# A causal mask added in PSUM by VectorE instead of by TensorE, and an output stage cut in the middle

## The chip, the core and the metric

The kernel runs on one core of a Trainium2 chip. The metric is the device time of one execution in microseconds. The core has five engines, each with a queue of its own that is worked off in order: TensorE (PE in the profile; its weight loads are PEld), VectorE (DVE), ScalarE (ACT), GpSimd (POOL) and SyncE (SP), which issues the transfers (DMA). TensorE's products go to PSUM, which has eight banks of 512 float32 columns on 128 partitions; the other working memory is SBUF.

## What is computed

Two layers on 512 tokens of width 1024. Each layer normalises, modulates, projects the tokens once, runs three causal token mixers (A: sparse attention over top-k keys, B: sliding window, C: stick-breaking), gates and merges them, and adds the projected result to the stream. A last norm follows. The change is in mixer C and in the end of the last layer. From the reference, cut down:

```python
def stick_breaking_attention(q, k, v):       # A[t,s] = beta_ts * prod_{s<j<t}(1-beta_tj), s < t
    ...
    strict = (key_pos[None, :] < qpos[:, None])[None, None]
    z = jnp.einsum('bthd,bshd->bhts', qb, k) * (dh ** -0.5)
    log_beta = jax.nn.log_sigmoid(z)
    log_1m = jnp.where(strict, jax.nn.log_sigmoid(-z), 0.0)
    after = lax.cumsum(log_1m, axis=3, reverse=True) - log_1m
    a = jnp.where(strict, jnp.exp(log_beta + after), 0.0)
    return jnp.einsum('bhts,bshd->bthd', a, v)
...
for l in range(DEPTH):
    h = hybrid_layer(h, ...)                 # ends in x + gate * (merged @ w_out)
return rms_norm(h, final_g)
```

Mixer C has 8 heads of width 64.

## The kernel before

All activations lie transposed, features on partitions and tokens in the free dimension. A float32 product is made of three products of rounded operands (high by high, high by low, low by high), so each 128 x 512 output tile of a projection from 1024 features takes 24 products (`ttile`), collected in a `ps_z` bank (3 of them). Weights come by DMA to `wstage` and are split into `whi` and `wlo` by VectorE, ScalarE or GpSimd.

**Order of the work.** The program is first written down by generators that are woven together (`Weave`, `SPACE` holds the spacing constants), and not issued. `Recorder` keeps every operation with the engines that could do it. Its `price` (line 337) gives each a cost per engine, `forward` (410) runs a list schedule over the five engines and the limited buffers, `latest` (544) works back when each operation has to run, which sets the priorities of the next round, and `order` (572) keeps the best of five rounds. `emit` issues that order; so nearly every instruction has line 596 in the profile, and the packed products line 594. The queue of each engine is therefore fixed when the kernel is built; at run time an instruction waits for its operands, and everything behind it on its engine waits too.

**Mixer C** (`c_qk`, 1166) works on pairs of heads, four pairs a layer. For one pair the scores of all four query blocks of 128 fill five `ps_s` banks (of which there are five): a bank per head for block 3 (512 keys), a bank per head for blocks 2 and 0 (384 and 128), and one for block 1 of both (`apos`). TensorE makes eight score products, one correction for the low parts, and seven packed ones (`low_parts`, 64 rows each); for pairs 1 to 3 the value products of the pair before ride in the same run (`value_run`). Before the change each score product was followed by a product of a bf16 identity with a bf16 mask, which adds -2^100 where a key is not before its query, on the last 128 columns. Then, for each bank: absolute value (ScalarE or VectorE), two ScalarE functions, VectorE's min-and-subtract, VectorE's scan from the right, an exponential on ScalarE. `softmax_tr` (1303) transposes the result on TensorE (20 pieces of 128 x 128 into five `ps_s` banks), and a copy brings each bank to SBUF. The next pair needs those five banks again. In the same stage run the projections of the coming pairs, the weight splits, and the top-k search of mixer A (`MAX`, `MATCH_REPLACE` on `score`), which only mixer A needs.

**Mixer A** has the same score code without a mask product (its mask is added by VectorE when a bank is read).

**The end** (`out_phase`, 1463). Output tiles 0 to 5 are computed at full width; tiles 6 and 7 in two parts along the tokens, 320 and 192 in the last layer. `update` adds the product to the old stream (`xm`), squares, collects the squares in `m2` (tile name `m`), and scales by the final gain. `after` forms the norm: a product with minus ones sums over partitions (`rstd`), ScalarE takes logarithm and exponential, once into PSUM for VectorE and once into `zs` for GpSimd; then eight multiplies per part (tiles 2 and 4 on GpSimd, the others on VectorE) and the stores, eight for the first part and four for the second.

**Constants.** `load_consts` (1612) brings rope tables, masks and the bf16 identity and mask at about 47 us.

## Time and profile before

| | us |
|---|---|
| median of 3 runs (lowest, highest) | 1167.84 (1166.76, 1167.96) |
| profiled execution | 1167.66 |
| its span, first to last instruction | 1165.8 |
| TensorE busy | 1154.7 |
| VectorE busy | 969.6 |
| ScalarE busy | 546.6 |
| GpSimd busy | 148.1 |
| granted TensorE clock, mean | 0.999 |

A busy TensorE is not one at its peak: products are pipelined, so the duration of one is longer than the distance to the next, and that distance is what a product costs in a stream. In a timeline row the columns are start, length of the group, engine, line, operation, out<-in, shapes and count; a bracket tells how long the engine sat idle before, and what ended that. Tile names have no buffer numbers: all score banks are `ps_s`.

### The profile page before, as it was taken

Reading aid. Unit: us, or ns where it says so; the run is one execution under the profiler, and the core shown is the slowest. Engines: PE = TensorE matmul, PEld = TensorE weight load, DVE = VectorE, ACT = ScalarE, POOL = GpSimd, SP = SyncE. Lnnn points to the kernel's source line nnn. Section 1 sums busy time; section 2 is a strip of 40 time slices with the busy share of each in tenths; the row PEclk is TensorE's granted clock in tenths of the full one; section 3 lists DMA queues with packets and bytes.
Section 4 is the critical chain, followed back from the end, with each engine's and each line's share of the span. In section 5 each row is a group of like instructions: output and inputs, shape, how many; then the busy total and the mean of one; then the engine's idle time right before and its main releaser. Section 6 shows DMA issues by size and latency. Waiting matters only on the chain.

```text
span 1165.8 us, 17663 instructions
## 1 busy us (share of the span) xinstructions
PE 1154.7 (99%) x5955; PEld 964.1 (83%) x5955; DVE 969.6 (83%) x2221; ACT 546.6 (47%) x1151; POOL 148.1 (13%) x198
## 2 busy tenths in 40 slices
PE   8999999999999999999999999999999999999997
PEld 6899777888888887788889987778888888877886
DVE  7967999999898987778687599999998988566765
ACT  5623766652555642432134157664545665242222
POOL 0100343421000100000000015443100010000000
PEclk9999999999999999999999999999999999999999
DMA  9744322443334445356544432234333333333342
GB/s 350 231 117 122 100 73 82 115 118 111 109 111 124 128 139 142 96 131 180 167 120 110 125 100 82 82 91 125 110 100 107 95 90 100 100 83 91 100 128 98
DMA packets 80539, 139.40 MB, mean 120 GB/s; under 512 B 10048, under 2 KB 20544, under 8 KB 80448
## 3 DMA queue, kind: packets, MB, share of 16 engines
q1 hardware_dynamic: 79296, 136.17, 40.2%
q10 hardware_dynamic: 1152, 2.10, 0.5%
q8 instruction: 47, 0.77, 0.3%
q14 instruction: 44, 0.36, 0.1%
HBM read 125.39 MB, written 4.19 MB: 111 GB/s over the span
## 4 chain that ended last, share of the span: by engine, by line
PE 98%; DVE 1%; DMA 1%; SPq 0%; ACT 0%; issue 0%; DVEq 0%
PE ps_z L596 74%; PE ps_s L596 19%; PE ps_s L594 4%; PE ps_z L594 2%; DMA Y<-in_w_ss 1%; DVE t L596 0%; SPq L596 0%; DVE Y L596 0%; DVE xm L596 0%; DVE e L596 0%; DVE wlo L596 0%; ACT zs L596 0%; DVE whi L596 0%; DVE m L596 0%; ACT ps_s L596 0%
## 5 line engine op out<-in xcount | busy, mean ns | idle before, releaser
L596 PE MATMUL ps_z<-uh,whi 128*128 128x512 f32 (+1 forms) x905 | 355.0, 394 | 0.0
L596 PE MATMUL ps_z<-uh,wlo 128*128 128x512 f32 (+1 forms) x905 | 351.9, 390 | 0.0
L596 PE MATMUL ps_z<-ul,whi 128*128 128x512 f32 (+1 forms) x905 | 351.2, 389 | 0.0
L596 DVE TENSOR_TENSOR wlo<-wstage,whi 128x512 fp32r<-128x512 f32 (+2 forms) x299 | 195.4, 656 | 14.3 <-ACT whi L596 4.9
L596 PEld LDWEIGHTS ps_z<-uh,wlo 128*128 128x128 f32 x905 | 169.9, 188 | 34.9 <-issue 0.7
L596 PEld LDWEIGHTS ps_z<-uh,whi 128*128 128x128 f32 x905 | 169.8, 188 | 34.8 <-issue 1.7
L596 PEld LDWEIGHTS ps_z<-ul,whi 128*128 128x128 f32 x905 | 169.9, 188 | 33.2 <-issue 0.3
L596 DVE CAST whi<-wstage 128x512 fp32r<-128x512 f32 (+2 forms) x215 | 88.0, 410 | 124.3 <-PE ps_z L596 103.8
L596 POOL TENSOR_TENSOR wlo<-wstage,whi 128x512 fp32r<-128x512 f32 (+2 forms) x73 | 93.4, 1282 | 391.9 <-DVE whi L596 87.5
L596 ACT CAST whi<-wstage 128x512 fp32r<-128x512 f32 (+1 forms) x124 | 74.1, 602 | 143.4 <-PE ps_z L596 128.9
L596 PE MATMUL ps_z<-Y,whi 128*128 128x512 f32 x384 | 119.1, 391 | 0.0
L596 ACT ACTIVATE e<-ps_z 128x512 f32<-128x512 f32 x68 | 40.5, 595 | 121.3 <-PE ps_z L596 121.0
L596 PEld LDWEIGHTS ps_z<-Y,whi 128*128 128x128 f32 x384 | 71.6, 188 | 14.6
L596 ACT ACTIVATE t<-t 128x512 f32<-128x512 f32 x120 | 69.4, 626 | 17.7 <-DVE t L596 16.8
L596 ACT ACTIVATE e<-e 128x512 f32<-128x512 f32 x96 | 59.8, 631 | 36.5 <-DVE e L596 36.0
L596 PE MATMUL ps_z<-Y,wlo 128*128 128x512 f32 x192 | 74.8, 389 | 0.0
L596 ACT ACTIVATE t<-t,nm 128x256 f32<-128x256 f32 (+3 forms) x128 | 65.0, 510 | 9.8 <-DVE nm L596 9.7
L596 PEld LDWEIGHTS ps_s<-small,t 128*128 128x128 f32 x432 | 50.4, 140 | 7.4
L596 PE MATMUL ps_s<-small,t 128*128 128x128 f32 x432 | 56.3, 273 | 0.0
L596 DVE MAX8 m<-score 128x8 f32<-128x256 f32 (+2 forms) x96 | 53.1, 555 | 1.2
L596 DVE MATCH_REPLACE8 score<-m,score 128x256 f32<-128x256 f32 (+2 forms) x96 | 52.0, 542 | 0.0
L596 PE MATMUL ps_s<-KH,Q 128*128 128x256 f32 (+3 forms) x280 | 50.6, 308 | 0.0
(219 smaller groups left out, 1938.3 us busy)
## 6 DMA issues: line engine op xcount, KB each, us to landing
wstage<-in_w_t SPq DMA_DIRECT2D x212, 256.0 KB, 2.7
wstage<-in_w_v SPq DMA_DIRECT2D x48, 182.0 KB, 2.4
m<-zs SPq DMA_DIRECT2D x128, 64.0 KB, 2.0
wstage<-in_w_gt SPq DMA_DIRECT2D x32, 256.0 KB, 2.7
wstage<-in_w_ss SPq DMA_DIRECT2D x32, 256.0 KB, 2.7
wstage<-in_w_o SPq DMA_DIRECT2D x32, 256.0 KB, 2.7
Y<-in_w_ss SPq DMA_DIRECT2D x15, 512.0 KB, 5.7
wstage<-in_w_first SPq DMA_DIRECT2D x16, 256.0 KB, 3.9
```

Of the source, the lines that this page charges most:

```text
L594: self.real[engine].matmul(*[real(a) for a in q[:3]], start=q[3], stop=True, skip_group_check=True)
L596: made = getattr(self.real[engine], y.op)(*[real(a) for a in y.args], **{k: real(v) for k, v in y.kw.items()})
```

## The change

1. Mixer C: the eight mask products of each block go. Instead VectorE adds the float32 mask to the bank in PSUM, in front of the absolute value: 128 columns for the two banks of block 3, 256 for the two banks of blocks 2 and 0 (their masked columns are neighbours), and two times 128 for the bank of block 1. The bf16 identity and mask, their casts and one staging tile go; the float32 mask is loaded to a tile of its own.
2. The end of the last layer: the parts are 256 and 256. The eight multiplies of a part are a function of their own (`last`). Those of the first part are recorded behind the updates of the second part, those of the second part at the very end. The first part uses GpSimd for tiles 1, 3 and 5 and buffers `Y`; both parts store two tiles with one transfer, four transfers each.
3. The planner: a product of under about 235 columns is priced at 0.112 us at least; a store to the output no longer holds up later transfers in the model; and the latest start of an operation counts its full latency.

```diff
-                c = 4 * n / 2.4e3 + 0.01 if rhs.dtype == F32 else 0.06 if rhs.dtype == BF16 else (n + 33.5) / 2.4e3
+                c = 4 * n / 2.4e3 + 0.01 if rhs.dtype == F32 else 0.06 if rhs.dtype == BF16 else max(0.112, (n + 33.5) / 2.4e3)
...
-                x.end = dma_free = max(at + (2.1 if at < 20.0 else 3.0), dma_free) + y.lag * (1.2 if dma_free < 5.5 else 1.0)
+                if not x.writes:
+                    x.end = at + 2.1
+                else:
+                    x.end = dma_free = max(at + (2.1 if at < 20.0 else 3.0), dma_free) + y.lag * (1.2 if dma_free < 5.5 else 1.0)
...
-        late = {x.i: end - x.hold for x in out}
+        late = {x.i: end - max(x.hold, x.end - x.start) for x in out}
...
                 for e in range(2):
                     mm(o[e], q[:, e, ts], kh[:, e, :W], first[e])
-                for e in range(2):
-                    mm(o[e][:, W - 128:], ident_b, cmask_b, False)
                 if i == 1:
                     mm(o[1], q[:, 1, ts], kl[:, S:], False)
             low_parts(q, kl, apos, zb, "c", p, LOW_ALL)
             for bk in (0, 3, 1, 4, 2):
                 z = zb[bk]
+                if bk % 3:
+                    m = z[:, 256:].rearrange("p (a b) -> p a b", a=2) if bk != 2 else z.rearrange("p (a b) -> p a b", a=2)[:, :, 128:]
+                    DVE.tensor_tensor(out=m, in0=m, in1=cmask.unsqueeze(1).to_broadcast([P, 2, P]), op=OP.add)
+                else:
+                    DVE.tensor_tensor(out=z[:, 384:], in0=z[:, 384:], in1=cmask, op=OP.add)
                 t = pt[bk] = t512("t", 10)
...
+        def last(cs_):
             w = cs_.stop - cs_.start
             for d in range(KT):
-                if d % 2 == 0 or w > S // 2:
-                    o, n = t512("t", 10), 0
-                v, a = o[:, n:n + w], st["xn"][d][:, cs_]
-                n += w
-                if d in (2, 4):
+                if d % 2 == 0:
+                    o = rec.tile("Y", [P, 2 * S], F32) if cs_.start == 0 else t512("t", 10)
+                v, a = o[:, w * (d % 2):w * (d % 2) + w], st["xn"][d][:, cs_]
+                if d in ((1, 3, 5) if cs_.start == 0 else (2, 4)):
                     POOL.tensor_tensor(out=v, in0=a, in1=st["rstd_sb"][:, cs_], op=OP.mult)
                 else:
                     DVE.tensor_tensor(out=v, in0=a, in1=st["rstd"][:, cs_], op=OP.mult)
-                if w > S // 2:
-                    SP.dma_start(out[:, d, cs_], v)
-                elif d % 2:
-                    SP.dma_start(out[:, d - 1:d + 1, cs_], o[:, :n].rearrange("p (a b) -> p a b", a=2))
+                if d % 2:
+                    SP.dma_start(out[:, d - 1:d + 1, cs_], o[:, :2 * w].rearrange("p (a b) -> p a b", a=2))
...
-            for cs_ in HALVES if l + 1 < L else (slice(0, 320), slice(320, S)):
+            parts = HALVES if l + 1 < L else (slice(0, 256), slice(256, S))
+            for cs_ in parts:
                 for i in range(2):
                     mms(6 + i, ws[2 * i:2 * i + 2], z[i], cs_)
                     update(6 + i, z[i], xr[i], cs_)
+                if cs_.start and l + 1 == L:
+                    last(parts[0])
                 after(cs_)
+            if l + 1 == L:
+                last(parts[1])
```

How the planner's order moves, at three places.

TensorE's queue at the first score block of mixer C in layer 0, before and then changed (`KH` keys, `Q` queries, `klow` low parts, `ps_z` a projection that runs around the block):

```order
L596 MATMUL ps_z_1370<-uh3_370,wlo_1300 128x512
L596 MATMUL ps_s_1397<-KH_1375,Q_1323 128x512
L596 MATMUL ps_s_1399<-KH_1375,Q_1323 128x512
L596 LDWEIGHTS ident_b_86
L596 MATMUL ps_s_1397<-cmask_b_87,ident_b_86 128x128
```

```order
L599 MATMUL ps_z_1366<-uh3_368,wlo_1296 128x512
L599 MATMUL ps_s_1393<-KH_1371,Q_1319 128x512
L599 MATMUL ps_s_1395<-KH_1371,Q_1319 128x512
L599 MATMUL ps_s_1398<-KH_1371,Q_1319 128x384
L599 MATMUL ps_s_1400<-KH_1371,Q_1319 128x384
L599 MATMUL ps_s_1398<-KH_1371,Q_1319 128x128
L599 MATMUL ps_s_1400<-KH_1371,Q_1319 128x128
L599 MATMUL ps_s_1409<-KH_1371,Q_1319 128x256 x2
```

The mask products, two behind each pair of score products, are gone; nothing else in the block moved but the correction with `klow`, which now follows the packed ones.

VectorE's queue behind the second score block of the same layer, before and then changed (`e` the gated value products of the pair before, `Y` its split, rows with 128x511 the scans):

```order
L596 TENSOR_TENSOR e_1686<-ps_z_1664,G_649 128x512
L596 TENSOR_SCALAR t_1692<-ps_s_1633 128x512
L596 TENSOR_SCALAR t_1700<-ps_s_1635 128x512
L596 TENSOR_TENSOR Y_1695<-e_1686,Y_1695 128x512
L596 TENSOR_SCALAR t_1712<-ps_s_1646 128x512
L596 SCALAR_TENSOR_TENSOR t_1683<-ps_s_1622,t_1683 128x512
L596 SCALAR_TENSOR_TENSOR t_1690<-ps_s_1624,t_1690 128x512
L596 MEMSET t_1683 128x1
L596 SCALAR_TENSOR_TENSOR t_1683<-ps_s_1622,t_1683 128x511
```

```order
L599 TENSOR_TENSOR e_1663<-ps_z_1637,G_645 128x512
L599 TENSOR_TENSOR ps_s_1608<-ps_s_1608,cmask_86 128x128
L599 CAST Y_1670<-e_1663 128x512
L599 TENSOR_TENSOR ps_s_1612<-ps_s_1612,cmask_86 128x128
L599 TENSOR_TENSOR Y_1670<-e_1663,Y_1670 128x512
L599 TENSOR_TENSOR ps_s_1614<-ps_s_1614,cmask_86 128x256
L599 TENSOR_TENSOR ps_s_1619<-ps_s_1619,cmask_86 128x256
L599 TENSOR_SCALAR t_1694<-ps_s_1614 128x512
L599 TENSOR_SCALAR t_1700<-ps_s_1619 128x512
L599 SCALAR_TENSOR_TENSOR t_1672<-ps_s_1608,t_1672 128x512
L599 SCALAR_TENSOR_TENSOR t_1681<-ps_s_1612,t_1681 128x512
L599 SCALAR_TENSOR_TENSOR t_1672<-ps_s_1608,t_1672 128x511
```

Four additions stand ahead of the first scan; the fifth (128x2x128) comes behind the fourth scan, with two search steps, a replacement and two low parts of keys between it and the last scan. From `e` to the last scan there are 17 rows before and 25 now. On TensorE the last four transposes of this block now stand behind 21 more products in three runs, where it was five in two, and 3 products ahead of the next block, where it was 19.

VectorE's queue at the end of the kernel, before and then changed (`xm_12108` and `xm_12079` are tile 7, `xm_12077` and `xm_12049` tile 6):

```order
L596 TENSOR_TENSOR m2_11831<-m2_11831,e_12148 128x192
L596 TENSOR_TENSOR t_12159<-xm0_11824,ps_s_12132 128x320
L596 TENSOR_TENSOR t_12168<-xm1_11868,ps_s_12132 128x320
L596 TENSOR_TENSOR t_12175<-xm3_11958,ps_s_12132 128x320
L596 TENSOR_TENSOR t_12182<-xm5_12043,ps_s_12132 128x320
L596 TENSOR_TENSOR t_12185<-xm6_12077,ps_s_12132 128x320
L596 TENSOR_TENSOR t_12188<-xm7_12108,ps_s_12132 128x320
L596 SCALAR_TENSOR_TENSOR xm7_12108<-ps_z_12074,mods1_77,G_12054 128x192
L596 TENSOR_TENSOR e_12195<-xm7_12108 128x192
```

```order
L599 TENSOR_TENSOR Y_12114<-xm0_11796,ps_s_12098 128x256
L599 SCALAR_TENSOR_TENSOR xm6_12049<-ps_z_12011,mods1_77,G_11982 128x256
L599 TENSOR_TENSOR Y_12124<-xm2_11885,ps_s_12098 128x256
L599 TENSOR_TENSOR Y_12130<-xm4_11973,ps_s_12098 128x256
L599 TENSOR_TENSOR Y_12138<-xm6_12049,ps_s_12098 128x256
L599 TENSOR_TENSOR Y_12138<-xm7_12079,ps_s_12098 128x256
L599 TENSOR_TENSOR m2_11803<-m2_11803,e_12127 128x256
L599 SCALAR_TENSOR_TENSOR xm7_12079<-ps_z_12046,mods1_77,G_12027 128x256
L599 TENSOR_SCALAR xm7_12079<-xm7_12079,small_69 128x256
```

The first part's multiplies on VectorE are five instead of six, and four of them now stand behind the second part's update of tile 6; the square of the last tile is no longer on VectorE. On TensorE the product that sums the first norm stands behind 63 of the 96 products of tiles 6 and 7, where it stood behind 69.

More of the change, by code (lines that the diff above doesn't have):

```diff
@@ L1608, in start @@
         ada_load(2)
-    sin_t = cos_t = tri0 = band = ident_b = cmask_b = None
+    sin_t = cos_t = tri0 = band = cmask = None
     def load_consts():
-        nonlocal sin_t, cos_t, tri0, band, ident_b, cmask_b
+        nonlocal sin_t, cos_t, tri0, band, cmask
         late = f(st["uh"][4][:, 0:1])
@@ L1622, in load_consts @@
         tri0, band = cb[:, 0:512], cb[:, 512:768]
-        cc = t512("t", 10)[:, :128]
-        POOL.tensor_copy(out=cc[:, 0:1], in_=late)
-        SP.dma_start(cc, consts[:, 768:896])
-        ident_b = fixed("ident_b", [P, P], BF16)
-        POOL.tensor_copy(out=ident_b, in_=ident)
-        cmask_b = fixed("cmask_b", [P, P], BF16)
-        POOL.tensor_copy(out=cmask_b, in_=cc[:, :P])
+        cmask = fixed("cmask", [P, P], F32)
+        POOL.tensor_copy(out=cmask[:, 0:1], in_=late)
+        SP.dma_start(cmask, consts[:, 768:896])
     def one(fn):
```

## The prediction, made before the changed kernel ran

> **What bounds the kernel now.** I read the busy shares on the first page of the profile, then the chain that ended last.
>
> ```profile
> PE 1154.7 (99%) x5955; PEld 964.1 (83%) x5955; DVE 969.6 (83%) x2221; ACT 546.6 (47%) x1151; POOL 148.1 (13%) x198
> PE 98%; DVE 1%; DMA 1%; SPq 0%; ACT 0%; issue 0%; DVEq 0%
> ```
>
> TensorE is busy for 1154.7 of 1165.8 us, and 98% of the chain runs through it. Idle time is left at the start and in the last 9 us. So a microsecond taken from TensorE's stream is a microsecond gained, as long as nothing else begins to make it wait. VectorE gets the new work, so I asked for busy time in stretches of 20 us: the second stick-breaking block, the sliding-window mixer after it, and the end.
>
> ```profile
> 140.00:160.00 20.00, 20.00 (x115) 15.60 (x114) 19.76 (x39) 14.80 (x27) 9.09 (x16) 1.00 0.34 94
> 300.00:320.00 20.00, 20.00 (x97) 16.76 (x96) 16.25 (x45) 12.49 (x34) 1.29 (x1) 1.00 0.40 119
> ```
>
> The columns are TensorE, its weight loads, VectorE, ScalarE, GpSimd, then the granted clock (1.00). In the stick-breaking stage VectorE has 0.24 us free in 20. It is full, though TensorE does not wait for it: much of what it does there is due later. That is the danger of this change: work goes from the engine that bounds the kernel to the one that has no room at that very place.
>
> **The mask products on TensorE.** The sparse mixer's score block is the same code shape without the mask: eight score products, one low part of 256 columns, seven packed low parts. The chain of waits in order of time has both, first a stick-breaking block (17 instructions ahead of the packed ones), then a sparse one (9); columns are start and length in us.
>
> ```profile
> 140.88 2.06 PE ps_s L596 x17
> 143.72 2.30 PE ps_z L594 x16
> 342.10 1.38 PE ps_s L596 x9
> 344.26 16.54 PE ps_z L596 x72
> ```
>
> From block start to the first instruction after the packed low parts: 2.84 us with the mask (140.88 to 143.72), 2.16 without (342.10 to 344.26). Eight mask products cost 0.68 us, and there are eight blocks (4 head pairs, 2 layers): **-5.4 us**. Bounds: at most 5.6 if a block varies by 0.02; nothing at all if TensorE comes to wait for VectorE at these places (a rival below). The nearest group row prices it otherwise:
>
> ```profile
> L596 PE MATMUL ps_s<-cmask_b,ident_b 128*128 128x128 bf16 x64 | 9.1, 224 | 0.0
> ```
>
> 224 ns is the latency of one pipelined product; 64 of them would be 14 us, which the block comparison rules out. The Trainium skill (TensorE: Matmul & The Clock Gate, Back-to-back issue gap) gives 56 ns from start to start for an isolated 128-column bf16 product and about 81 ns in a stream with weight loads; an estimate from that page for 64 products is 3.6 to 5.2 us. By the page the sum below would come out 0.2 to 1.8 us smaller; the block comparison exceeds both, as it also holds what the change of type costs its neighbours.
>
> **More interruptions by transposes.** In the changed order 63 runs of transposes stand between other products, where 58 stood. What one costs shows behind the second block's scans:
>
> ```profile
> 156.98 1.58 PE L596 MATMUL ps_s<-small,t 128*128 128x128 f32 x13
> 158.31 0.48 PE L596 MATMUL ps_z<-uh,whi 128*128 128x512 f32 x1
> 159.09 0.49 PE L596 MATMUL ps_s<-small,t 128*128 128x128 f32 x3
> 159.34 0.47 PE L596 MATMUL ps_z<-uh,whi 128*128 128x512 f32 x1
> 159.66 0.40 PE L596 MATMUL ps_z<-ul,whi 128*128 128x512 f32 x1
> 159.89 0.60 PE L596 MATMUL ps_s<-small,t 128*128 128x128 f32 x4
> 164.66 0.61 PE L596 MATMUL ps_s<-KH,Q 128*128 128x512 f32 x2
> ```
>
> The product behind a run lasts 0.32 us from start to start (159.34 to 159.66) where its neighbours take 0.23 (159.66 to 159.89). Five more runs by 0.09: **+0.45 us**.
>
> **The additions on VectorE.** 16 additions of 128 columns and 24 of 256 (16 in one piece, 8 in two), read from PSUM and written to PSUM. No VectorE instruction of this kind is in the trace. The nearest rows, one with a PSUM operand and 256 columns, the other a masked maximum out of PSUM of 128:
>
> ```profile
> L596 DVE TENSOR_TENSOR xm<-xm,ps_s 128x256 f32<-128x256 f32 x4 | 1.5, 417 | 2.3 <-ACT ps_s L596 2.3
> L596 DVE CUSTOM_DVE_ANT_0 t<-ps_s,cb 128x128 f32<-128x128 f32 x32 | 8.1, 287 | 0.0
> ```
>
> Alone they would take 24 x 0.417 + 16 x 0.287 = 14.6 us; in a row, where instructions overlap by 0.08, 11.2. I take 0.34 and 0.20 each, 1.4 us per block; the upper bound is that writing PSUM costs as much again. What hides 11 to 15 us? Total: VectorE has 196 us free, but not here. It makes room by deferring the top-k search, which shares this stage:
>
> ```profile
> L596 DVE MATCH_REPLACE8 score<-m,score x45: 400/543/679, 123.0 to 296.0; 128x384 f32<-128x384 f32 x16, 128x512 f32<-128x512 f32 x16, 128x256 f32<-128x256 f32 x13
> L596 DVE CUSTOM_DVE_ANT_0 t<-ps_s,score x2: 686/686/687, 343.9 to 344.6; 128x512 f32<-128x512 f32 x2
> ```
>
> The search ends at 296.0 and its result is first read at 343.9. The order moves its last row from 496 to 524 of VectorE's list, and the reader from 604 to 609: 85 rows remain between. Besides, GpSimd gets 23 rows more and ScalarE 14, with weight splits taken off VectorE. So the total costs nothing; without that slack it would be up to 14.6 us.
>
> What can cost is latency. Each addition stands in front of everything done to its bank, and in three of the four blocks of a layer the first one stands behind `e<-ps_z,G` on VectorE's queue, which waits for the previous pair's value products. Queued behind are the four other additions, the five scans, and so the transposes. For the second block I set the two engines against each other: in one timeline TensorE's first product behind the value products, and VectorE's `e` and last scan; and from the groups the exponential behind a scan and the copy behind transposes.
>
> ```profile
> 145.95 0.50 PE L596 MATMUL ps_z<-uh,whi 128*128 128x512 f32 x1
> 146.07 0.69 DVE L596 TENSOR_TENSOR e<-ps_z,G 128x512 f32<-128x512 f32 x1
> 157.12 1.20 DVE L596 TENSOR_TENSOR_SCAN t<-ps_s,t 128x511 f32<-128x511 f32 x1
> ...
> L596 ACT ACTIVATE t<-t 128x512 f32<-128x512 f32 x120 | 69.4, 626 | 17.7 <-DVE t L596 16.8
> L596 DVE COPY t<-ps_s 128x512 f32<-128x512 f32 x30 | 20.3, 684 | 0.2
> ```
>
> From `e` to the end of the last scan: 12.25 us. The new order has in this stretch five additions (1.4), a cast and two search rows and one replacement (0.35 each, an estimate from the 0.4 of such instructions less the overlap), and one more key low part (0.6); a memset (0.1) goes to GpSimd: 15.5 us. The exponential behind the last scan takes 0.63, hand-overs 0.2: the last four transposes may run 16.3 us after `e` starts. TensorE starts its products 0.12 us ahead of `e` (145.95). In the new order it does 48 of them (11.0 us: the old order has the same 48 ahead of 156.98), ten transposes (1.0), then 21 products in three runs with two times three transposes between them (21 x 0.227 + 3 x 0.09 + 0.5 = 5.5): it reaches the last four 17.4 us after `e` starts, 1.1 us later than they can be had. Before, the same four came at 159.89 and the next block not until 164.66; now that block follows 0.7 us of products behind them, and its last bank is wanted another 1.0 us later, with one copy (0.7) between. The ring is closed without stall, but with about 1 us of room where there were 4. I allow **+0.3 us** for places where it does not fit; the bounds are 0 and 8 x 0.5.
>
> **The end.** The last output tiles were cut 320 + 192, and are now cut 256 + 256. Rates first: 256-column products in the first layer's end, 320 and 192 in the second's.
>
> ```profile
> 577.78 0.28 PE L596 MATMUL ps_z<-vc,wlo 128*128 128x256 f32 x1
> 581.38 0.28 PE L596 MATMUL ps_z<-va,wlo 128*128 128x256 f32 x1
> 1144.17 0.30 PE L596 MATMUL ps_z<-vc,whi 128*128 128x320 f32 x1
> 1151.06 0.31 PE L596 MATMUL ps_z<-va,wlo 128*128 128x320 f32 x1
> 1153.52 0.72 PE L596 MATMUL ps_s<-m,nones 128*128 128x320 f32 x2
> 1154.18 0.27 PE L596 MATMUL ps_z<-KH,whi 128*128 128x192 f32 x1
> 1156.97 0.27 PE L596 MATMUL ps_z<-va,wlo 128*128 128x192 f32 x1
> ```
>
> 3.60 us / 30 = 0.120 for 256; 6.89 / 47 = 0.147 for 320; 2.79 / 25 = 0.112 for 192, hardly less than for 256. 48 of each: 12.4 us before, 96 x 0.120 = 11.5 after. From the stage's first product at 1144.17 the last one started 12.8 us later. Now 63 products (7.56), the norm's sum (0.5 with re-entry) and 32 more (3.84) put it at 11.9, its end at 12.2. Then:
>
> ```profile
> 1155.72 2.47 DVE L596 TENSOR_TENSOR t<-xm,ps_s 128x320 f32<-128x320 f32 x6
> 1158.10 0.41 DVE L596 SCALAR_TENSOR_TENSOR xm<-ps_z,mods,G 128x192 f32<-128x192 f32 x1
> 1160.41 1.68 DVE L596 TENSOR_TENSOR t<-xm,ps_s 128x192 f32<-128x192 f32 x6 [1.15 <-ACT ps_s L596]
> 1160.85 1.14 POOL L596 TENSOR_TENSOR t<-xm,zs 128x192 f32<-128x192 f32 x2 [3.18 <-ACT zs L596]
> L596 SPq DMA_DIRECT2D out<-t x12: 338/411/458, 1156.2 to 1162.6; - x12
> ```
>
> The last update ran at 1158.10, 13.9 us after 1144.17, though its product had ended 0.86 us earlier: six multiplies of the first part stood ahead of it. In the new order the update starts at 12.3: five multiplies of 0.33 and two updates fit ahead of it while TensorE finishes. That is 1.6 us won. Given back: update, square, norm sum, logarithm and exponential on 256 instead of 192 columns, 0.05 to 0.06 each (update 0.41 for 192 against 0.47 by the slope of the six multiplies, 0.40 apart at 320 and 0.27 at 192), 0.3 in all; GpSimd's two multiplies, 0.55 apart at 192 and so 0.69 at 256, gate the third store, 0.3; the last store carries 256 KB for 192, about 0.2. Sum: **-0.8 us**, bounds -0.2 (stores limited by bandwidth) and -1.4 (stores not on the path). The first half's stores go out some 3 us ahead of the others and cost nothing; without that distance they would share the bandwidth, which is in the bounds.
>
> The constants' load (one transfer, two small casts fewer on GpSimd at 3 and 47 us) lies beside busy TensorE: nothing.
>
> Sum: -5.4 + 0.45 + 0.3 - 0.8 = -5.5 us. The profiled execution took 1167.66 (span 1165.8 and 1.86 around it), so 1162.2; the median of the runs is 0.18 higher: **1162.4 us**.
>
> **The rivals.**
>
> *The ring of a stick-breaking block decides at times.* The additions stretch the chain beyond the 1.1 us of room, or the new order, drawn with the same spacing constants as the old, leaves TensorE waiting elsewhere. 0.1 to 0.4 us in each of eight blocks takes back 1 to 3 us: 1163.5 to 1165.5. For it: VectorE full, a block's last transposes put behind three more microseconds of products. Against: the old order has such places too, without a visible wait.
>
> The Trainium skill (VectorE: DVE Perf Modes, The DRAIN you can't avoid) says that the next VectorE instruction does not start until the pipeline is empty; then an addition would hold the queue for its whole 0.29 or 0.42. The six multiplies, 0.48 us long and 0.40 apart, do not show that; by it the chain grows 0.4 us, still inside the room, and the time would stay.
>
> *The mask products were not on the path after all.* If the chain of a block, not TensorE, sets its pace, only the end is gained: about 1167. Against: 20.00 busy of 20.00, no wait in the stage.
>
> *Slower.* An addition into PSUM costs over 0.65 us instead of 0.28 on average, and the chain of a block grows by 1.85 us beyond my count: 1.1 of room and 0.75 of stall. From there the gain is gone (8 x 0.75 = 6), and each further 0.25 us costs 2: at twice that stall 1168 + 6 = 1174. Only the missing PSUM-write row speaks for it; reads of PSUM in every other row price an operand normally.
>
> **How the numbers follow.** Forecast as summed, 1160.6 to 1163.5: 0.64. Ring decides at times: 0.17. Only the end gained, or all taken back: 0.11. Slower: 0.08. A change under 0.2% (2.3 us) cannot be told from none, so faster is 0.81, same 0.11, slower 0.08. The range reaches from 1160.6 (no stall, most of the bounds) to 1166.0, leaving out the slower cases and the worst of the third.
>
> **What would show it.** Right: blocks of 17 instructions become 9 in 1.4 us, 2.2 us to the next product; TensorE busy near 1149 us with no wait on transposes or score banks; additions near 0.42 and 0.29 us; the search's last row later than 296; the last update within 0.1 us of its product, and 96 products 0.120 apart. Wrong: gaps in TensorE ahead of the last transposes or of the next block's score products (rival one), a score block as long as before, additions beyond 0.6 us, or a last store more than 0.6 us later against the last product than now.

## The result and the profile after

The changed kernel takes 1161.41 us (median of 6 runs, 1161.13 to 1162.57) beside 1167.7 for the kernel before in the same series: a ratio of 0.9948, 95% interval 0.9938 to 0.9959. The forecast was 1162.4. In the run with the mask alone (below), one of the five executions, the profiled one, took 2336.38 us; it is left out, so that run has a time but no lengths. The profiled execution has a span of 1159.7 us where it was 1165.8, so 6.1 us less. Busy times and the shares of the chain, from the first page of the profile after:

```profile
PE 1148.5 (99%) x5891; PEld 960.7 (83%) x5891; DVE 965.7 (83%) x2222; ACT 550.9 (48%) x1165; POOL 170.4 (15%) x221
PE 98%; DVE 1%; ACT 0%; DMA 0%; issue 0%; SPq 0%; DVEq 0%
```

TensorE has 6.2 us less to do and still ends everything. VectorE, which got 40 additions, is busy for 3.9 us less than before: the planner moved work away from it, weight splits above all (9.7 us by the sum of their durations), and GpSimd is up by 22.3 us, 13.9 of it weight splits, ScalarE by 4.3.

The chain of waits in order of time gives landmarks that both kernels have (start, length): the end of the head (`x99`, the value projections of each layer), a stick-breaking block, and the first long run of the sparse mixer (`x72`). First those of before that the prediction did not show, then after:

```profile
55.75 16.76 PE ps_s L596 x99
626.01 16.76 PE ps_s L596 x99
914.53 16.54 PE ps_z L596 x72
```

```profile
55.44 16.77 PE ps_s L599 x99
139.88 1.39 PE ps_s L599 x9
142.06 2.30 PE ps_z L597 x16
339.35 1.38 PE ps_s L599 x9
341.51 16.54 PE ps_z L599 x72
623.29 16.77 PE ps_s L599 x99
909.46 16.54 PE ps_z L599 x72
```

A stick-breaking block now has 9 instructions ahead of the packed ones and is 2.18 us long to the next product (139.88 to 142.06), as a sparse one is (339.35 to 341.51, 2.16). Starts taken from each other give lengths by stretch; the end is counted from the first product of tile 6 (1144.17 before, 1139.12 after) to the end of the span.

| stretch | before | after | change |
|---|---|---|---|
| head, to the value projections | 55.75 | 55.44 | -0.31 |
| layer 1, from there to the sparse mixer's long run | 288.51 | 286.07 | -2.44 |
| layer 2, the same | 288.52 | 286.17 | -2.35 |
| between these stretches | 511.39 | 511.44 | +0.05 |
| end, from tile 6's first part on | 21.63 | 20.58 | -1.05 |

The two mixer stretches hold 4.8 of the 6.1 us, the end 1.05. The head ran from 55.44 to 56.29 over the profiles of this case. It follows VectorE's first group of six (`Y`), which starts 44.3 to 44.4 us earlier, between 11.0 and 11.9, when the load of `in_w_ss` lands; so its 0.31 is not put down to the change.

The additions (the view of one tile's instructions; columns are shortest, median and longest in ns, then first and last start):

```profile
L599 DVE TENSOR_TENSOR ps_s<-ps_s,cmask x40: 289/409/429, 124.1 to 770.0; 128x256 f32<-128x256 f32 x24, 128x128 f32<-128x128 f32 x16
```

Writing to PSUM costs nothing extra: 0.41 us for 256 columns and 0.29 for 128, as the reading rows said. The search whose delay was to pay for them, in the same view:

```profile
L599 DVE MATCH_REPLACE8 score<-m,score x45: 402/543/678, 122.7 to 293.9; 128x384 f32<-128x384 f32 x16, 128x512 f32<-128x512 f32 x16, 128x256 f32<-128x256 f32 x13
```

Its last row is at 293.9, against 296.0 before. All of the program is 2.7 us ahead by then, so the search is late by some 0.6 us and no more.

The ring of the second block, from the timelines of VectorE, ScalarE and TensorE:

```profile
144.86 0.69 DVE L599 TENSOR_TENSOR e<-ps_z,G 128x512 f32<-128x512 f32 x1
145.47 0.29 DVE L599 TENSOR_TENSOR ps_s<-ps_s,cmask 128x128 f32<-128x128 f32 x1
145.67 0.42 DVE L599 CAST Y<-e 128x512 fp32r<-128x512 f32 x1
...
154.58 0.63 ACT L599 ACTIVATE t<-t 128x512 f32<-128x512 f32 x1 [1.17 <-DVE t L599]
155.33 1.25 PE L599 MATMUL ps_s<-small,t 128*128 128x128 f32 x10
156.97 0.62 ACT L599 ACTIVATE t<-t 128x512 f32<-128x512 f32 x1
157.49 0.58 ACT L599 COPY t<-ps_s 128x512 f32<-128x512 f32 x1
158.15 0.52 PE L599 MATMUL ps_s<-small,t 128*128 128x128 f32 x3
159.57 1.20 DVE L599 TENSOR_TENSOR_SCAN t<-ps_s,t 128x511 f32<-128x511 f32 x1
160.87 0.63 ACT L599 ACTIVATE t<-t 128x512 f32<-128x512 f32 x1 [0.80 <-DVE t L599]
161.95 0.60 PE L599 MATMUL ps_s<-small,t 128*128 128x128 f32 x4
```

Read pairwise. The exponential that ends at 155.21 lets ten transposes start at 155.33: 0.12 us between. The copy that ends at 158.07 frees the bank for the three at 158.15: 0.08 us. The exponential that ends at 161.50 lets the last four start at 161.95: 0.45 us. No wait of TensorE is shown in these rows, and none of the three pairs has a microsecond to spare.

The end of the kernel, TensorE, VectorE and the group of the last stores:

```profile
1139.12 0.28 PE L599 MATMUL ps_z<-vc,whi 128*128 128x256 f32 x1
1150.95 0.28 PE L599 MATMUL ps_z<-va,wlo 128*128 128x256 f32 x1
1151.26 0.48 DVE L599 SCALAR_TENSOR_TENSOR xm<-ps_z,mods,G 128x256 f32<-128x256 f32 x1
1153.91 2.08 DVE L599 TENSOR_TENSOR t<-xm,ps_s 128x256 f32<-128x256 f32 x6 [1.33 <-ACT ps_s L599]
L599 SPq DMA_DIRECT2D out<-t x4: 372/392/460, 1154.7 to 1156.3; - x4
```

The last update starts 0.03 us behind its product (1150.95 + 0.28), 12.14 us after the stage's first product where it was 13.93. The last multiplies start at 14.79 instead of 16.24, and the last store is issued at 17.2 instead of 18.4 and lands 3.4 us later (3.2 before).

### The profile page after: what moved, and what is told of

Its sections match the earlier page's. It is cut to its first block, busy times and chain, and to the rows that moved or that the text cites. A ratio compares the mean times of both kernels' runs of the same rounds, so it can differ in the third digit from the quotient of the medians.

```text
span 1159.7 us, 17599 instructions
## 1 busy us (share of the span) xinstructions
PE 1148.5 (99%) x5891; PEld 960.7 (83%) x5891; DVE 965.7 (83%) x2222; ACT 550.9 (48%) x1165; POOL 170.4 (15%) x221
## 4 chain that ended last, share of the span: by engine, by line
PE 98%; DVE 1%; ACT 0%; DMA 0%; issue 0%; SPq 0%; DVEq 0%
PE ps_z L599 74%; PE ps_s L599 18%; PE ps_s L597 4%; PE ps_z L597 2%; DMA vc<-in_xT 0%; ACT t L599 0%; DVE t L599 0%; DVE Y L599 0%; DVE wlo L599 0%; DVE xm L599 0%; ACT csr L599 0%; ACT zs L599 0%; ACT e L599 0%; DVE whi L599 0%; ACT ps_s L599 0%
## 5 line engine op out<-in xcount | busy, mean ns | idle before, releaser
L599 DVE TENSOR_TENSOR wlo<-wstage,whi 128x512 fp32r<-128x512 f32 (+2 forms) x292 | 190.9, 657 | 16.2 <-ACT whi L599 6.7
L599 DVE CAST whi<-wstage 128x512 fp32r<-128x512 f32 (+1 forms) x202 | 82.7, 410 | 122.4 <-PE ps_z L599 101.4
L599 POOL TENSOR_TENSOR wlo<-wstage,whi 128x512 fp32r<-128x512 f32 (+1 forms) x80 | 102.3, 1283 | 367.3 <-ACT whi L599 133.7
L599 ACT CAST whi<-wstage 128x512 fp32r<-128x512 f32 (+2 forms) x129 | 77.2, 603 | 128.5 <-PE ps_z L599 107.2
L599 ACT ACTIVATE t<-t,nm 128x256 f32<-128x256 f32 (+3 forms) x128 | 65.1, 510 | 11.5 <-DVE nm L599 11.4
L599 PE MATMUL ps_s<-wlo,uh 128*128 128x364 f32 x144 | 47.5, 330 | 0.0
```

Source lines behind the costliest of these rows:

```text
L599: made = getattr(self.real[engine], y.op)(*[real(a) for a in y.args], **{k: real(v) for k, v in y.kw.items()})
```

## Which part of the change made the gain

The change has three parts: the mask, the end, and three edits to the planner's prices. Three kernels take them apart; all have the planner's edits.

**The mask with the old end.**

```diff
-            parts = HALVES if l + 1 < L else (slice(0, 256), slice(256, S))
+            for cs_ in HALVES if l + 1 < L else (slice(0, 320), slice(320, S)):
...
```
(and `after` with its multiplies and stores as they were)

> The changed kernel with the old end (cut 320 + 192, multiplies of the first part recorded with its norm); its mixer stages are instruction for instruction those of the changed kernel. Theory (the mask products lay on TensorE's path, 0.66 us in each of eight blocks, less some 0.5 us for more runs of transposes): 4.8 us faster than before, 1162.9 us, and a tail of 21.6 us from the first product of tile 6 to the end. Rival (the gain is made in the end alone, the mixer only shifts waits): within 1 us of before, 1167 us.

Measured: 1162.6 us (four executions) beside 1167.65, ratio 0.9957 (0.9944 to 0.9971), so 5.0 us faster. Whether its end is 21.6 us long, as expected, was not measured. On every engine its order is that of the changed kernel up to the last two output tiles. The mixers make the gain; the rival that held the mask products to be off the path is out.

**The new end with the mask products.**

```diff
+                for e in range(2):
+                    mm(o[e][:, W - 128:], ident_b, cmask_b, False)
...
-                    DVE.tensor_tensor(out=m, in0=m, in1=cmask..., op=OP.add)
```

> The old mask products with the new end (cut 256 + 256, multiplies of the first part recorded last), and the planner's three new rules. Theory: 1.0 us faster than before, 1166.7 us, tail of 20.6 us from the first product of tile 6. Rival (the end's gain exists only with the VectorE freed elsewhere): within 0.3 us of before.

Measured: 1167.14 us beside 1167.65, ratio 0.9994 (0.9985 to 1.0003): 0.5 us, not told from none. Its profile explains why it is less than 1.0: the end is 20.52 us long, as expected, but the second layer's stretch is 288.85 instead of 288.52, and in this execution the head took 0.42 more (56.17). By its length the end's gain is there without the mask's change, against the rival; the times alone could not tell.

**The planner's three edits alone.**

```diff
-                c = ... else (n + 33.5) / 2.4e3
+                c = ... else max(0.112, (n + 33.5) / 2.4e3)
-                x.end = dma_free = max(...) + y.lag * ...
+                if not x.writes:
+                    x.end = at + 2.1
-        late = {x.i: end - x.hold for x in out}
+        late = {x.i: end - max(x.hold, x.end - x.start) for x in out}
```

> The planner's three new rules alone (floor of 0.112 us on a packed product, no queueing of stores, later due times for DMAs); masks and end as before. They move weight splits between VectorE, GpSimd and ScalarE. Theory: TensorE's stream has the same instructions, so within 0.5 us of before, 1167.7 us. Rival: the 0.3 us that the changed kernel is ahead in the head, before the first score block, and part of the mixer's gain come from these rules: 0.3 to 2 us faster.

Measured: 1167.92 us, ratio 1.0005 (0.9996 to 1.0014). The same time, but not the same schedule. The end in its timelines of GpSimd and VectorE:

```profile
1155.43 0.51 POOL L599 TENSOR_TENSOR e<-xm 128x192 f32<-128x192 f32 x1 [176.41 <-DVE xm L599]
1155.20 2.47 DVE L599 TENSOR_TENSOR t<-xm,ps_s 128x320 f32<-128x320 f32 x6
1157.59 0.35 DVE L599 TENSOR_TENSOR m<-m,e 128x192 f32<-128x192 f32 x1
1157.85 0.41 DVE L599 SCALAR_TENSOR_TENSOR xm<-ps_z,mods,G 128x192 f32<-128x192 f32 x1
1160.16 1.68 DVE L599 TENSOR_TENSOR t<-xm,ps_s 128x192 f32<-128x192 f32 x6 [1.15 <-ACT ps_s L599]
```

One square of the last part has gone to GpSimd (the first row), so the update comes 13.52 us after the stage's start (1144.33) instead of 13.93, and the end is 21.17 us, 0.46 shorter. The second layer's stretch is 0.30 longer. The two nearly cancel. In the changed kernel the loss in the second layer hardly appears (286.17, with 286.07 in the first). Of its 1.05 at the end, up to 0.46 may be due to these edits, which the prediction had not priced; no run has the new end without them, so that share is not shown.

**The two halves of the new end.** One kernel keeps the cut at 256 and records the first part's multiplies early as before, with the old assignment too (GpSimd has tiles 2 and 4, buffers `t`); the other keeps them last and moves the cut back to 320; a third moves it to 272. The first edit is shown in part.

```diff
-                if d in ((1, 3, 5) if cs_.start == 0 else (2, 4)):
...
+                if d in (2, 4):
...
-                if cs_.start and l + 1 == L:
-                    last(parts[0])
```

> The changed kernel with the cut at 256 + 256 kept, but the first part's multiplies recorded right behind its norm, ahead of the second part's last square, as before. Theory (the planner's priorities, not the place in the record, set VectorE's order; what counts for the update is that it stands behind none of the multiplies): if the update of tile 7 is again behind the multiplies it starts up to 1 us late, and the kernel is 0.3 to 1 us slower than the changed one. Rival (the cut alone makes the gain): within 0.2 us of the changed kernel.

```diff
-            parts = HALVES if l + 1 < L else (slice(0, 256), slice(256, S))
+            parts = HALVES if l + 1 < L else (slice(0, 320), slice(320, S))
```

> The changed kernel with the cut moved back to 320 + 192, the first part's multiplies still recorded last and stored in pairs. Theory: the products take 12.4 us instead of 11.5, 0.9 us more; given back are the shorter norm, multiplies and last store of 192 columns, about 0.6 us: 0.2 to 0.5 us slower than the changed kernel. Rival (the update freed of the multiplies is the whole gain): same as the changed kernel or up to 0.6 us faster.

```diff
+            parts = HALVES if l + 1 < L else (slice(0, 272), slice(272, S))
```

> The changed kernel with the cut at 272 + 240. TensorE's time for the 96 products is the same by a price linear in columns (0.127 + 0.113 against two times 0.120), the norm, multiplies and last store get 16 columns less, 0.15 us in all. Theory: 0.0 to 0.3 us faster than the changed kernel, not to be told from it. Rival (the first part's stores or multiplies come in the way): 0.2 us or more slower.

| kernel | median | ratio to before (95%) | end in the profile |
|---|---|---|---|
| changed | 1161.41 | 0.9948 (0.9938 to 0.9959) | 20.58 |
| cut 256, multiplies early | 1161.85 | 0.9946 (0.9932 to 0.9959) | 20.80 |
| cut 320, multiplies last | 1162.11 | 0.9948 (0.9935 to 0.9960) | 20.73 |
| cut 272, multiplies last | 1161.89 | 0.9947 (0.9935 to 0.9960) | 20.69 |

The times do not tell the four apart. The lengths of the end do: in the five runs below that end as the changed kernel does (those without additions and with more of them) it is within 0.05 us of 20.58. By them each half alone keeps most of the gain, and is 0.15 to 0.22 behind the two together; 0.15 is just under the 0.2 to 0.5 expected for the cut at 320. With the early multiplies VectorE still reaches the last update soon enough:

```profile
1148.53 2.08 DVE L599 TENSOR_TENSOR t<-xm,ps_s 128x256 f32<-128x256 f32 x6 [1.78 <-ACT ps_s L599]
1150.52 0.48 DVE L599 SCALAR_TENSOR_TENSOR xm<-ps_z,mods,G 128x256 f32<-128x256 f32 x1
1151.48 0.43 DVE L599 TENSOR_TENSOR m<-m,e 128x256 f32<-128x256 f32 x1 [0.48 <-ACT e L599]
1151.83 0.48 DVE L599 SCALAR_TENSOR_TENSOR xm<-ps_z,mods,G 128x256 f32<-128x256 f32 x1
```

The first of the two updates is tile 6, late because of the six multiplies ahead of it; a wait for its square stands between it and tile 7, whose update starts 12.43 us after the stage's start (1139.40), 0.29 later than in the changed kernel. So the expected loss of 0.3 to 1 us is 0.2 by the profile. Moving the cut on to 272, from which 0.0 to 0.3 us was expected, brings nothing (20.69).

## What the mask products cost, and whether the additions are free

**The products left out, everything else in the old order.**

```diff
                 y = x.alts[engine]
+                if y.op == "matmul" and y.args[2].dtype == BF16:
+                    continue
```

> The kernel before, in its own order, with the 64 mask products simply not issued: the mask of the stick-breaking mixer is left out. Theory (0.68 us per block on TensorE's path): 5.4 us faster, 1162.3 us, blocks 2.16 us long instead of 2.84. By the page-derived price of 56 to 81 ns per product: 3.6 to 5.2 us. Rival (the blocks' chain sets the pace, TensorE only waits longer elsewhere): under 1.5 us faster.

Measured: 1163.67 us, ratio 0.9966 (0.9954 to 0.9979), so 4.0 us faster: less than the price of the blocks. That 4.0 lies in the second range of the expectation (3.6 to 5.2) is luck: the blocks did become 0.66 us shorter each, as the theory had it (2.92 to 2.26 from the first score product to the first value product), and something else takes part of it back.

By the same landmarks the stretches are 286.28 (55.73 to 342.01) and 286.57 (623.76 to 910.33), 2.23 and 1.95 shorter than before; the changed kernel wins 2.44 and 2.35. From one score block to the next the third and the fourth block come 0.61 and 0.54 sooner than before (first layer), but the second only 0.43, in the second layer 0.13. Where it is taken back shows in TensorE's timeline behind the first block, before and then with the products left out:

```profile
133.73 0.40 PE L596 MATMUL ps_z<-uh,wlo 128*128 128x512 f32 x1
133.97 0.38 PE L596 MATMUL ps_s<-small,t 128*128 128x128 f32 x2
```

```profile
133.04 0.40 PE L598 MATMUL ps_z<-uh,wlo 128*128 128x512 f32 x1
133.43 0.30 PE L598 MATMUL ps_s<-small,t 128*128 128x128 f32 x1
```

The transpose starts 0.24 us behind the product ahead of it in the one, 0.39 in the other. TensorE now arrives at it before VectorE's scan, for which it waits, has ended (133.28). No wait is printed, because the product's own 0.40 us covers the gap. Summed over all runs of transposes in the two stretches, such delays come to 0.8 us. In the second layer's first block the correction with `klow` is late as well: it comes 0.30 us behind the product ahead of it, where it is 0.12 in the first layer. So the old order, made for the longer blocks, holds part of the gain back, and a new order by the planner frees it: the mixers win 4.8 us with the additions on VectorE, and 4.2 without any mask in the old order.

**The additions left out, the changed kernel's order kept.**

```diff
+                if y.op == "tensor_tensor" and y.kw["in1"].tile is tiny[1]:
+                    continue
```
(`tiny[1]` is the mask's tile)

> The changed kernel in its own order with the 40 additions on VectorE not issued: the mask of the stick-breaking mixer is left out. Theory (the additions are hidden, the ring of a block has about 1.1 us of room): same time as the changed kernel within 0.5 us, 1161.4 us. Rival (the ring decides at times): 1 to 3 us faster than the changed kernel, 1158.5 to 1160.5 us.

Measured: 1162.38 us, ratio 0.9955 (0.9942 to 0.9967), beside 0.9948 for the changed kernel. The stretches are 286.02 (55.69 to 341.71) and 286.51 (623.50 to 910.01), against 286.07 and 286.17 with the additions. Product by product, TensorE is nowhere in the two stretches more than 0.05 us ahead of where it is with the additions. Nothing is won by taking the additions away: in this order they are free, and the rival, as far as it lays the loss on the additions, is out. That the order itself makes TensorE wait a little is not touched by this run.

## How much room the ring has

That 40 additions cost nothing does not say that the next ones would. Here one, then two more of the same shape that add zeros are issued at each; the order of all else is kept. In the queue they stand ahead of the mask's addition, not behind it as the expectations say, which makes no difference to what waits for the bank.

```diff
+                if y.op == "tensor_tensor" and y.kw["in1"].tile is tiny[1]:
+                    zero = ...
+                    for _ in range(1):
+                        self.real[engine].tensor_tensor(out=real(y.kw["out"]), in0=real(y.kw["in0"]), in1=real(zero), op=OP.add)
                 made = ...
```
(`range(2)` in the second run)

> The changed kernel in its own order with each of the 40 additions followed by a second one of the same shape that adds zeros: 1.4 to 1.8 us more on VectorE ahead of a block's last scan. Theory (room of about 1.1 us in the ring of a block, from then on a stall of the full excess): 0.3 to 0.7 us of stall in each of eight blocks, 2.4 to 5.6 us slower than the changed kernel, 1163.8 to 1167.0 us. Rival one (the room is several us, TensorE's queue always has work): within 0.5 us of the changed kernel. Rival two (no room at all): 11 to 14 us slower.

> As the run with doubled additions, with two zero additions behind each: 2.8 to 3.6 us more on VectorE per block. Theory (room 1.1 us): 1.7 to 2.5 us of stall per block, 14 to 20 us slower than the changed kernel. Rival one (room of several us): under 3 us slower. Rival two (no room): 22 to 29 us slower.

Measured: 1176.91 us doubled, ratio to the kernel before 1.0078 (1.0064 to 1.0092), and 1196.28 us tripled, 1.0244 (1.0230 to 1.0258). That is 15.5 and 34.9 us slower than the changed kernel. The expected room of 1.1 us per block is wrong, and so is the rival of several; the figure of "no room at all" is even exceeded. The tripled run is not the ring alone, though: in its profile the granted clock fell to 0.50 four times, for some 3.4 us each (from 136.5, 163.85, 191.1 and 720.2 us), which in the changed kernel's mixers it does not. The first three lie in the first layer, whose stretch is 17.65 us longer, the fourth in the second, with 15.80 (doubled, the two are 7.53 and 7.51 longer); by that difference each costs about 0.9 us, and the four together some 4 of the 34.9, an estimate. TensorE's and VectorE's timelines of the second block with the additions doubled:

```profile
148.39 0.29 DVE L602 TENSOR_TENSOR ps_s<-ps_s,cb 128x128 f32<-128x128 f32 x1
148.72 0.30 DVE L603 TENSOR_TENSOR ps_s<-ps_s,cmask 128x128 f32<-128x128 f32 x1
148.92 0.42 DVE L603 CAST Y<-e 128x512 fp32r<-128x512 f32 x1
...
158.02 0.27 PE L603 MATMUL ps_s<-small,t 128*128 128x128 f32 x1
159.79 1.20 PE L603 MATMUL ps_s<-small,t 128*128 128x128 f32 x9 [1.50 <-ACT t L603]
163.03 0.55 PE L603 MATMUL ps_s<-small,t 128*128 128x128 f32 x3 [0.31 <-ACT t L603]
166.84 0.60 PE L603 MATMUL ps_s<-small,t 128*128 128x128 f32 x4
```

TensorE waits 1.50 us at the first ten transposes and 0.31 at the second three (by the spacing of starts it loses 0.16 more at each), and not at all at the last four, the one place that the prediction had worked out. The price of an added instruction is higher too: an addition that depends on the one ahead of it starts 0.33 us later (148.39 to 148.72), an independent instruction 0.20 later (148.72 to 148.92).

That gave a new theory: the edge lies at the two pairs with 0.12 and 0.08 us between. The first depends on the first four additions, the second on the fifth, by way of ScalarE's queue: the copy that frees the bank stands behind the fifth bank's function. Two kernels load one of the two each.

```diff
+                if ... is tiny[1] and not (tuple(y.kw["out"].shape) == (P, 2, P) and y.kw["out"].at.strides[1] == 256):
...
+                    for _ in range(1):
```
(one zero addition at each of additions 1 to 4 of a block; the condition leaves out the fifth)

> The changed kernel in its own order with one zero addition more behind each of the first four additions of a block, none at the fifth: by the trace with all doubled, 2 x 0.33 + 2 x 0.46 = 1.6 us more ahead of the exponential that the first ten transposes wait for. New theory (the edge of the ring is at those ten transposes: in the changed kernel the exponential ends at 155.21 and they start at 155.33, room 0.1 us): 1.4 to 1.5 us of stall in each of eight blocks, 11 to 12 us slower than the changed kernel, 1172.5 to 1173.5 us. Old theory (1.1 us of room, at the last four transposes): 0.5 us per block, 4 us slower, 1165.5 us.

```diff
+                if ... is tiny[1] and (tuple(y.kw["out"].shape) == (P, 2, P) and y.kw["out"].at.strides[1] == 256):
...
+                    for _ in range(2):
```
(two zero additions at the fifth alone)

> The changed kernel in its own order with two zero additions more at the fifth addition of a block alone: 0.9 us more behind the fourth scan and ahead of the fifth. New theory (at the last four transposes the changed kernel has 0.4 us: the exponential ends at 161.50, they start at 161.95): 0.4 to 0.5 us of stall per block, 3 to 4 us slower than the changed kernel, 1164.5 to 1165.5 us. Old theory (1.1 us of room there): same as the changed kernel within 0.5 us. A third (no room there either): 7 us slower.

The first: 1173.85 us, ratio 1.0050 (1.0036 to 1.0064), 12.4 us slower than the changed kernel (11 to 12 expected); its two stretches are 5.65 and 5.88 longer, 1.44 us a block, the rest is in the head. The second: 1167.77 us, ratio 1.0000 (0.9991 to 1.0008), 6.4 us slower; 3.00 and 2.99 in its stretches, 0.75 a block. I had expected 3 to 4, from the 0.45 us at the last four transposes; the 7 of the third case came nearer. The wait is elsewhere again, in the second block's timelines of ScalarE and TensorE:

```profile
158.87 0.63 ACT L603 ACTIVATE t<-t 128x512 f32<-128x512 f32 x1 [0.70 <-DVE t L603]
159.40 0.57 ACT L603 COPY t<-ps_s 128x512 f32<-128x512 f32 x1
160.02 0.55 PE L603 MATMUL ps_s<-small,t 128*128 128x128 f32 x3 [0.63 <-ACT t L603]
```

ScalarE stands 0.70 us waiting for the fifth bank's absolute value from VectorE, with the copy queued behind; three transposes wait for that copy. Some 0.9 us more on VectorE, less the 0.08 of room, is the 0.8 us that this block loses. It does not explain all eight: they lose between 0.55 and 1.10 us each, always ahead of transposes, but what ends the waits printed there is at times VectorE, and those pairs were not worked out. I had named this pair when I read the doubled run, and still took the expectation from the wrong one.

## Why the prediction was right, point by point

- **What bounds.** Right: TensorE's products taken away shorten the time (5.0 us with the mask alone).
- **Mask products, -5.4.** The block went from 2.84 to 2.18 us, so 0.66 x 8 = 5.3. Right. 0.66 us for eight is 82 ns each; the Trainium skill (TensorE: Matmul & The Clock Gate, Back-to-back issue gap) has about 81 in a stream with weight loads and 56 isolated, so this trace agrees with its stream figure, but only as an average. Two mask products take 0.09 us from start to start (122.19 to 122.28 below), and the two score products behind them 0.44 (to 122.72), where in the changed kernel they take 0.35 (121.88 to 122.23): some 0.4 of the 0.66 us is the mask products' own (four times 0.09), the rest falls on their neighbours.

```profile
122.19 0.29 PE L596 MATMUL ps_s<-cmask_b,ident_b 128*128 128x128 bf16 x2
122.28 0.60 PE L596 MATMUL ps_s<-KH,Q 128*128 128x384 f32 x2
122.72 0.29 PE L596 MATMUL ps_s<-cmask_b,ident_b 128*128 128x128 bf16 x2
```

- **More runs of transposes, +0.45, and stalls, +0.3.** Together 0.75, and 0.62 came of it, but this agreement is luck, for the step behind the 0.45 is wrong. Take for each run of transposes in the two mixer stretches the time from the start of the product ahead of it to that of the second product behind it, less two products of 0.227. The sum is 30.69 us before (46 runs) and 31.31 after (51 runs, the same 272 transposes); all else in TensorE's stream is 5.41 shorter, which is the 5.4 of the mask. By this count a run of 1 takes 0.12 at the least, one of 3 0.33, one of 14 1.54: about 0.11 a transpose, so a run as such costs next to nothing. A lone transpose in the changed kernel shows why:

```profile
208.82 0.39 PE L599 MATMUL ps_z<-ul,whi 128*128 128x512 f32 x1
209.05 0.27 PE L599 MATMUL ps_s<-small,t 128*128 128x128 f32 x1
209.08 0.47 PE L599 MATMUL ps_z<-uh,wlo 128*128 128x512 f32 x1
209.39 0.39 PE L599 MATMUL ps_z<-uh,whi 128*128 128x512 f32 x1
```

The product behind a run does take 0.31 instead of 0.23, as the prediction read, but it starts 0.03 behind the last transpose, which elsewhere takes 0.11. At these prices five more runs are under 0.1 us. The other 0.5 to 0.6 us are delays of single runs beyond these least times, too short to be printed as waits. They are there without the additions too (31.42), so the new order makes them, not the additions: this is the second half of the rival by which the ring decides at times, at a fifth to a half of its price.

- **The additions.** Durations right, 0.41 and 0.29 (its 11.2 us in a row is 11.4 by its own figures, which changes nothing). "What hides them" was half right: the search gave way by 0.6 us only, not by pushing its last row past 296.0. By the busy times the cover is rather the 22.3 us of work that GpSimd took, 13.9 of it weight splits; the prediction had named these second.
- **The ring, "about 1 us of room".** This step failed. It was worked out for the last four transposes alone, and there it came out as 0.45 us measured (161.50 to 161.95) for 1.1 estimated: the last scan ended 0.4 later and TensorE arrived 0.3 earlier than counted. The first ten and the second three were never set against their chains, and they have 0.12 and 0.08 us. The forecast held because in the second block the planner had set every piece just in time, not because there was slack.
- **The slower rival, "over 0.65 us an addition".** The point from which it decides lay far closer: one more addition at each place, 0.33 to 0.46 us, already costs 15.5 us, more than the whole gain.
- **The DRAIN rule.** The sum by the Trainium skill (VectorE: DVE Perf Modes, The DRAIN you can't avoid) was said to cost the chain 0.4 us "inside the room". There was no such room, so by that rule the kernel would have lost some 2 us, an estimate from the page's rule (eight blocks by the 0.4 less 0.12). The trace does not show it between independent instructions (145.47 to 145.67, 0.20 us for one of 0.29 us), but does between dependent ones (0.33).
- **The end, -0.8.** Measured -1.05. The update came 1.79 us earlier relative to its stage (1.6 forecast), and 0.74 was given back (0.8). The attribution was too simple: the planner's edits alone shorten the end by 0.46, and with them each half of the new end by itself brings the length within 0.25 of the changed kernel's.

## What to carry to other kernels

Where work is moved to an engine whose results others wait for in order, set every consumer in the ring against its producer, not only the last one, and look at what stands in the queue behind the delayed instruction on a third engine. A printed profile without waits does not mean slack: measure it by adding harmless work at one place, which here cost 0.75 or 1.44 us a block (1.9 at all places) while taking work away gained nothing. And where a forecast comes out, check its terms one by one: here a wrong term and an allowance covered each other. When instructions are removed from a fixed order, have the order made anew: it was worth 0.6 us of 4.8 here.

## What the runs showed that was not expected

TensorE can wait up to about 0.2 us without a wait being printed, since a 512-column product is 0.39 us long and the next starts 0.23 behind it; such waits show only as spacing (0.39 for 0.24). And two VectorE additions on the same bank that depend on each other start 0.33 us apart at 128 columns, with 0.29 for the instruction itself, while the independent one behind them follows after 0.20; in that place the dependent pair costs about 1.6 times what an independent one does.

A bf16 product between the others delays more than itself: with two mask products ahead of them, the two score products of 384 columns take 0.44 us from start to start instead of 0.35. And a run of transposes has no fixed price in TensorE's stream: 0.11 us a transpose, whether 1, 3 or 14 stand together.
